# A two-layer encoder on one core: transfers, buffers and the order of products around a saturated TensorE

## The chip, the core and the metric

The kernel runs on one core of a Trainium2 chip. The metric is the device time of one execution in microseconds. Three runs of the kernel before gave 1870.45 us in the median (1870.34 to 1870.78).

## The reference, cut to what matters

Two layers of a macaron encoder over 512 tokens of width 1024, in float32: a half-step feed-forward part, gated parallel mixers (neighbourhood attention and a Fourier mix), a second half-step feed-forward part, and a norm at the very end.

```python
def swiglu(x, w_in, w_out):
    gu = x @ w_in
    g, u = jnp.split(gu, 2, axis=-1)
    return (jax.nn.silu(g) * u) @ w_out

def mixer(h, w_in, gate_bias, rpb, w_na_out, w_f_out, w_o):
    z = h @ w_in
...
    y_na = neighbourhood_attention(q.reshape(shp), k.reshape(shp), v.reshape(shp), rpb) @ w_na_out
    y_f = fourier_mix(uf) @ w_f_out
    g_na = jax.nn.sigmoid(ga + gate_bias[0])
    g_f = jax.nn.sigmoid(gf + gate_bias[1])
    return (g_na * y_na + g_f * y_f) @ w_o

def reference(x, ...):
    for l in range(DEPTH):
        x = x + 0.5 * swiglu(rms_norm(x, ffn1_norm[l]), ffn1_w_in[l], ffn1_w_out[l])
        x = x + mixer(rms_norm(x, mix_norm[l]), ...)
        x = x + 0.5 * swiglu(rms_norm(x, ffn2_norm[l]), ffn2_w_in[l], ffn2_w_out[l])
    return rms_norm(x, final_norm)
```

## The kernel before

**Products.** Every float32 operand is split into a high part (rounded, `hi`) and a low part (the rest, `lo`), and a product is three matmuls: high by high, high by low, low by high. ScalarE makes the high part of a weight tile (`Item.upper`, lines 196 and 198), VectorE the low part (`Item.lower`, lines 203 and 205). Large products are done in seven instead of eight block products (Strassen-like): with weight quarters a, b, c, d the products are numbered 1 to 7: 1 uses -a, 2 uses b, 5 uses d + c, 6 adds a to that tile, 3 adds b, 7 uses c + a, 4 uses d alone. Product 6 and 3 thus go on with the tile that product 5 began.

**Weight stream.** `stage_items` lists all weight granules (128 x 1024 floats, 512 KB) in the order in which TensorE uses them; `Stream` walks the list. `Raw.load` (lines 150 to 159) issues a granule's plain load on SyncE's queue and, for each granule that is to be added, a transfer with accumulation on POOL's queue. `fetch` loads 8 (feed-forward and second half of a mixer) or 4 items ahead of `high`; `high` makes the high part (and a sum on VectorE, line 191, where the item has an `add`), `low` the low part, and, where the item has a `then`, a further accumulating transfer onto the raw tile behind its split (line 215). Raw tiles of the feed-forward stages come from a pool of 9 buffers (`ffn_raw`, line 1811), split tiles from pools of 3.

In the feed-forward stages the sums of products 6 and 3 are made on VectorE from granules loaded by themselves. In the mixer's gate and output projections (`dma=True`) they are made by accumulating transfers. The output projection (`ORDER_W`) has a tile `s` of its own for products 6 and 3, which is d with c and then a added by two accumulating transfers; there are two such tiles, one for each half of the rows.

**The mixer's gates.** Two blocks of products (`block`, `block_1`), one for each half of the gates' columns, run interleaved as generators; the order in which `next` is called (lines 1740 to 1760) must be that of the items (line 288): ends with block 0's 6 and 7, block 1's 5, block 0's 3 and 4, block 1's 6, 7, 4, 3.

**End of the last feed-forward stage.** The output product of a stage goes over three thirds c of the hidden width. In the last layer (`late`) product 4's activations are made by a negation on ScalarE (line 1022) and an accumulating transfer on POOL (line 1023, the tile `at`). After product 7 of the last third the order of PE, VectorE and ScalarE is written out by hand in `end_part`: product 3's last granules, product 4 over its three thirds with the activations split in place (`upper`, its `lower`, lines 909 and 911), and interleaved the updates of x (line 730), the squares for the final norm (line 412), its roots, and the final scaling: `gained` multiplies by the gain (line 1063), `scaled` by the inverse norm and sends (lines 1068, 1069), `whole` does both at once (lines 1073, 1074).

**Start.** `ws.fetch(1)` issues the first granule in two halves on ScalarE's queue, then a small Silu brings in its table, while SyncE's queue loads the transposed x (`xt`) in five pieces with further granules between them (lines 1834 to 1856).

Of the kernel before, what the change touches and what calls it, by code (L numbers as in the profile page):

```python
# [17 lines left out]
P = 128  # L18
D = 1024
T = 512  # L20
L = 2
# [74 lines left out]
def encoder_kernel(  # L96
# [48 lines left out]

    class Raw:
# [3 lines left out]
        def load(self, parts=1):  # L150
            if self.t is None:
                self.t = raw_pool[0](self.n)
                for c in range(0, self.n, self.n // parts):
                    cs = slice(c, c + self.n // parts)
                    (S if parts > 1 else nc.sync).dma_start(out=self.t[:, cs], in_=wst[GRAN_AT[self.key]][:, cs])
                for plus in self.plus:
                    z = G.dma_start(out=self.t, in_=wst[GRAN_AT[plus]][:, 0 : self.n], accum_op=ALU.add)  # L157
                    if self.key[1:] == ("gc", 1, 1):
                        tc.keep_in_program_order(z)

# [56 lines left out]
    def stage_items():  # L217
# [7 lines left out]
        def strassen(s, name, idx, sizes, order, dma=False):  # L225
# [9 lines left out]
            for m in order:  # L235
                for g in range(len(sizes)):
                    a, b, c, d = [r[q][g] for q in "abcd"]
                    if m == 1:
                        add(a, neg=True)
                    elif m == 2:  # L240
                        add(b)
                    elif m == 3:
                        add(r["s"][g] if "s" in r else d, None if dma else b)
                    elif m == 4:
                        add(d2[g])
                    elif m == 5:
# [10 lines left out]
        def ffn(s):  # L257
            first = not items
            for g in range(4):
                add(Raw((s, "cl", g)), parts=2 if first and g < 2 else 1, pieces=2 if first and g == 0 else 1)  # L260
            for j in range(NB):
                order = (1, 2, 5, 6, 7, 3, 4) if s == (0, 1) and j == 0 else (1, 5, 6, 2, 7, 3, 4)
                strassen(s, lambda q: q, j, (1024, 1024), order)
            for order in ((1,), (2,), (5, 6, 7, 3), (4,)):
                for c in range(3):
                    strassen(s, lambda q: "o" + q, c, out_sizes(c), order)

        for l in range(L):
# [19 lines left out]
            for i, order in ((0, (5,)), (1, (2,)), (0, (6, 7)), (1, (5,)), (0, (3, 4)), (1, (6, 7, 4, 3))):  # L288
# [319 lines left out]
    def stage_ffn(norm, nxt, late):  # L608
# [274 lines left out]
        def end_part(i):  # L883
# [33 lines left out]
            ws.high()  # L917
            nxt.squares(1, 1)
# [3 lines left out]
            lower = upper(i + 3)  # L922
# [10 lines left out]
            lower = upper(i + 4)  # L933
# [8 lines left out]
            lower()  # L942
# [14 lines left out]
            scaled(nxt, 2, 1)  # L957
            for z in chain:
# [9 lines left out]
            gained(3, 1)  # L968
# [3 lines left out]
            scaled(nxt, 3, 1)  # L972
# [14 lines left out]
        for i, (m, c, _) in enumerate(steps):  # L987
# [36 lines left out]
            if late and (m, c) == (7, 2):  # L1024
                end_part(i)
# [51 lines left out]
    def stage_mixer(l, norm, nxt):  # L1077
# [732 lines left out]
    def ffn_raw(n):  # L1810
        return scope_pool[0].tile([P, 1024], F32, tag="raw", name=nm("raw"), bufs=9)[:, 0:n]
# [22 lines left out]
    ws.fetch(1)  # L1834
    S.activation(small("rt", 1), ones, AF.Silu)
    with tc.manual_schedule(engines={mybir.EngineType.SP}):
        for kts in ((0,), (1,), (2, 3), (4, 5), (6, 7)):
# [8 lines left out]
            src = src.rearrange("p (a b) -> p a b", b=T)  # L1846
            ws.fetch(kts[-1] // 2 + 1)
# [183 lines left out]
```

## Time and profile before

| | us |
|---|---|
| median of three runs | 1870.45 |
| profiled execution, its own time | 1872.14 |
| its span, first to last instruction | 1870.4 |
| TensorE busy | 1858.8 |
| VectorE busy | 1491.6 |
| ScalarE busy | 1176.1 |
| POOL busy | 182.5 |

The granted clock was 0.999 in the mean. In a row of a timeline the first number is the start in us from the span's start, the second the duration; then engine, line, operation, tile written and tiles read, shapes and count; in brackets how long the engine was idle before it and what released it. PE is TensorE's matmuls, PEld its weight loads, DVE VectorE, ACT ScalarE, SPq, ACTq and POOLq the transfers that these engines issue. Rows of waits read: engine, tile and line that waited, what for, us in total, how often, longest.

### The profile page before, as it was taken

To read this page: it belongs to the slowest core of one execution; us is meant where nothing else is said; L and a number is where in the kernel's file an instruction comes from. 1 tells how busy PE (TensorE), PEld (TensorE's weight loads), DVE (VectorE), ACT (ScalarE), POOL (GpSimd) and SP (SyncE) were. 2 spreads that over 40 slices of the span, in tenths; PEclk is the share of its full clock that TensorE was granted. 3 is DMA by queue.
4 is the path that set the end of the run, shared out by engine and by line. 5 is a ranking of instruction groups with operands and counts; after the bars stand their busy time and mean duration, and the time that the engine had idled before them with its cause. 6 is when DMAs were issued, how large, how long until landed. Compare 5 with 4: busy or idle time off the path is not lost.

```text
span 1870.4 us, 25957 instructions
## 1 busy us (share of the span) xinstructions
PE 1858.8 (99%) x9609; PEld 1583.5 (85%) x9609; DVE 1491.6 (80%) x1831; ACT 1176.1 (63%) x1751; POOL 182.5 (10%) x219
## 2 busy tenths in 40 slices
PE   9999999999999999999999999999999999999998
PEld 7888888889998888888888888888899988888886
DVE  7777799758879777779967777996687787777898
ACT  6655665768657655566665556667676575555665
POOL 0101011100211000001000100101002110100010
PEclk9999999999999999999999999999999999999999
DMA  9777488774998477659857774979659885765695
GB/s 301 204 197 198 151 238 272 249 205 121 253 241 231 133 206 184 182 154 264 242 141 198 198 183 148 262 226 279 196 142 248 231 232 144 191 182 163 180 272 181
DMA packets 110319, 384.57 MB, mean 206 GB/s; under 512 B 12512, under 2 KB 12640, under 8 KB 110192
## 3 DMA queue, kind: packets, MB, share of 16 engines
q1 hardware_dynamic: 79952, 276.81, 42.1%
q0 software_dynamic: 29808, 105.32, 30.7%
q8 instruction: 75, 1.23, 0.3%
q10 hardware_dynamic: 432, 0.79, 0.1%
q14 instruction: 52, 0.43, 0.1%
HBM read 375.13 MB, written 6.29 MB: 204 GB/s over the span
## 4 chain that ended last, share of the span: by engine, by line
PE 93%; DMA 2%; DVE 2%; issue 1%; ACT 1%; POOL 0%; ACTq 0%; POOLq 0%; DVEq 0%
PE A L367 9%; PE A L370 9%; PE A L368 9%; PE o L370 7%; PE o L367 7%; PE o L368 7%; PE B L367 5%; PE B L368 5%; PE B L370 5%; PE ps L367 3%; PE ps L368 3%; PE ps L370 3%; PE C L367 2%; PE C L370 2%; PE C L368 2%; PE tr L624 2%
## 5 line engine op out<-in xcount | busy, mean ns | idle before, releaser
L205 DVE TENSOR_TENSOR wlo<-raw,whi 128x1024 fp32r<-128x1024 f32 (+2 forms) x524 | 619.1, 1189 | 227.0 <-ACT whi L198 224.5
L198 ACT ACTIVATE whi<-raw 128x1024 fp32r<-128x1024 f32 (+2 forms) x524 | 537.5, 1032 | 340.6 <-PE A L368 128.7
L157 POOL DMA_DIRECT2D raw<-in_wst_dram x170 | 147.3, 879 | 1434.0 <-DMA raw<-in_wst_dram 824.9
L191 DVE TENSOR_TENSOR raw<-raw,raw 128x1024 f32<-128x1024 f32 (+1 forms) x128 | 151.3, 1187 | 2.4
L367 PE MATMUL A<-whi,xh 128*128 128x512 f32 x320 | 124.5, 389 | 0.0
L368 PE MATMUL A<-whi,xl 128*128 128x512 f32 x320 | 124.5, 389 | 0.0
L705 ACT ACTIVATE th<-sn,r 128x512 f32<-128x512 f32 x80 | 57.0, 715 | 73.6 <-DVE sn L606 73.6
L196 ACT ACTIVATE whi<-raw 128x1024 fp32r<-128x1024 f32 x76 | 78.8, 1037 | 34.4 <-issue 17.1
L203 DVE SCALAR_TENSOR_TENSOR wlo<-raw,whi 128x1024 fp32r<-128x1024 f32 x76 | 90.5, 1190 | 8.1 <-ACT whi L196 8.0
L370 PE MATMUL A<-wlo,xh 128*128 128x512 f32 x320 | 92.1, 389 | 0.0
L601 ACT ACTIVATE sn<-A 128x512 f32<-128x512 f32 x96 | 56.1, 590 | 46.0 <-PE A L370 46.0
L368 PEld LDWEIGHTS A<-whi,xl 128*128 128x128 f32 x320 | 60.1, 188 | 12.5
L370 PEld LDWEIGHTS A<-wlo,xh 128*128 128x128 f32 x320 | 60.1, 188 | 12.5
L367 PEld LDWEIGHTS A<-whi,xh 128*128 128x128 f32 x320 | 60.1, 188 | 12.5
L367 PE MATMUL B<-whi,t1h 128*128 128x512 f32 x160 | 63.7, 398 | 0.0
L367 PE MATMUL A<-whi,t2h 128*128 128x512 f32 x160 | 62.5, 391 | 0.0
L367 PE MATMUL B<-whi,xh 128*128 128x512 f32 x160 | 62.4, 390 | 0.0
L368 PE MATMUL B<-whi,xl 128*128 128x512 f32 x160 | 62.3, 390 | 0.0
L368 PE MATMUL B<-whi,t1l 128*128 128x512 f32 x160 | 62.3, 390 | 0.0
L368 PE MATMUL A<-whi,t2l 128*128 128x512 f32 x160 | 62.3, 389 | 0.0
L368 PE MATMUL A<-whi,t3l 128*128 128x512 f32 x160 | 62.2, 389 | 0.0
L367 PE MATMUL C<-whi,xh 128*128 128x512 f32 x160 | 62.2, 389 | 0.0
(454 smaller groups left out, 4895.4 us busy)
## 6 DMA issues: line engine op xcount, KB each, us to landing
raw<-in_wst_dram SPq DMA_DIRECT2D x463, 512.0 KB
raw<-in_wst_dram POOLq DMA_DIRECT2D x184, 512.0 KB, 8.1
raw<-in_wst_dram SPq DMA_DIRECT2D x28, 256.0 KB
vc<-vd SPq DMA_DIRECT2D x28, 256.0 KB
bm<-in_near_dram SPq DMA_DIRECT2D x16, 384.0 KB
vd<-v SPq DMA_DIRECT2D x8, 512.0 KB
dft<-in_dft_dram POOLq DMA_DIRECT2D x4, 514.0 KB, 10.2
x<-in_xin_dram SPq DMA_DIRECT2D x4, 512.0 KB
```

The lines of the kernel that those rows point to most:

```text
L157: z = G.dma_start(out=self.t, in_=wst[GRAN_AT[plus]][:, 0 : self.n], accum_op=ALU.add)
L191: V.tensor_tensor(self.raw.t, self.raw.t, self.add.t, ALU.add)
L196: S.activation(self.out[0][:, cs], self.raw.t[:, cs], AF.Copy, scale=-1.0)
L198: S.activation(self.out[0][:, cs], self.raw.t[:, cs], AF.Copy)
L203: self.last = V.scalar_tensor_tensor(lo, t, -1.0, hi.bitcast(F32), ALU.mult, ALU.subtract)
L205: self.last = V.tensor_tensor(lo, t, hi.bitcast(F32), ALU.subtract)
L367: PE.matmul(ps, lh, rh, start=start, stop=False, skip_group_check=again)
L368: PE.matmul(ps, *((lh, rl) if w == "l" else (ll, rh)), start=False, stop=False, skip_group_check=again)
L370: PE.matmul(ps, *((ll, rh) if w == "l" else (lh, rl)), start=False, stop=stop, skip_group_check=again)
L601: S.activation(t[:, b, :], ps[b], AF.Copy)
L624: PE.transpose(tr[:, k, b * P : (b + 1) * P], a[:, b, (q + k) * P : (q + k + 1) * P], ident)
L705: S.activation(th[:, b, :], g[:, b, :], AF.Silu, scale=norm.r[:, c : c + 1])
```

## The change

- `Raw.load` issues only the first accumulating transfer at once; a second one is put off until the next raw tile that is loaded has issued its own first one (`pending`). Only the tiles `s` of the output projection have two.
- The first granule's first half goes out on SyncE's queue, behind the first piece of `xt`, its second half on ScalarE's queue, behind the small Silu.
- The raw pool has 10 buffers.
- In the last output product, last third (`end`), product 3's sum is made by an accumulating transfer behind product 6's split, instead of on VectorE.
- In both layers the gates' products end in another order: block 0's 6, block 1's 5, block 0's 7 and 3, block 1's 6, block 0's 4, block 1's 7, 4, 3.
- In `end_part` product 4's second activations are split before the hand-written order begins (`make(i + 3)`), its third ones behind the first granule of product 3; `gained` and `scaled` for token block 3 come before the last block of products.

```diff
+    pending = []
...
-                    (S if parts > 1 else nc.sync).dma_start(out=self.t[:, cs], in_=wst[GRAN_AT[self.key]][:, cs])
-                for plus in self.plus:
-                    z = G.dma_start(out=self.t, in_=wst[GRAN_AT[plus]][:, 0 : self.n], accum_op=ALU.add)
+                    (S if c and parts > 1 else nc.sync).dma_start(out=self.t[:, cs], in_=wst[GRAN_AT[self.key]][:, cs])
+                for plus in self.plus[0:1]:
+                    z = self.gather(plus)
                     if self.key[1:] == ("gc", 1, 1):
                         tc.keep_in_program_order(z)
+                while pending:
+                    raw, plus = pending.pop(0)
+                    raw.gather(plus)
+                pending.extend((self, plus) for plus in self.plus[1:])
+
+        def gather(self, plus):
+            return G.dma_start(out=self.t, in_=wst[GRAN_AT[plus]][:, 0 : self.n], accum_op=ALU.add)
...
-                        add(r["s"][g] if "s" in r else d, None if dma else b)
+                        add(r["s"][g] if "s" in r else d, None if dma or end else b)
...
-                        add(t, None if dma else a, then=b.key if dma else None)
+                        add(t, None if dma else a, then=b.key if dma or end else None)
...
-                    strassen(s, lambda q: "o" + q, c, out_sizes(c), order)
+                    strassen(s, lambda q: "o" + q, c, out_sizes(c), order, end=(*s, c) == (L - 1, 2, 2))
...
-            for i, order in ((0, (5,)), (1, (2,)), (0, (6, 7)), (1, (5,)), (0, (3, 4)), (1, (6, 7, 4, 3))):
+            for i, order in ((0, (5,)), (1, (2,)), (0, (6,)), (1, (5,)), (0, (7, 3)), (1, (6,)), (0, (4,)), (1, (7, 4, 3))):
...
             go(p3, i + 1, 0, w[0])
             ws.high()
+            lower = upper(i + 4)
             nxt.squares(1, 1)
             ws.low()
             ws.high()
             go(p3, i + 1, 1, w[1])
-            lower = upper(i + 3)
             update(ps[1], 0, 1, -1)
...
             go(p4, i + 2, 1, ws.next(0))
-            lower = upper(i + 4)
...
             go(p4, i + 3, 0, ws.next(0))
-            lower()
...
             gained(2, 1)
             scaled(nxt, 2, 1)
+            gained(3, 1)
+            scaled(nxt, 3, 1)
...
-            gained(3, 1)
             whole(nxt, 2, 0)
             whole(nxt, 3, 0)
             next(chain[0])
-            scaled(nxt, 3, 1)
...
             if late and (m, c) == (7, 2):
+                make(i + 3)
                 end_part(i)
...
         written.pop().__exit__(None, None, None)
+        next(block_1)
+        next(block)
         next(block)
         next(block_1)
-        next(block)
         next(block)
...
-        return scope_pool[0].tile([P, 1024], F32, tag="raw", name=nm("raw"), bufs=9)[:, 0:n]
+        return scope_pool[0].tile([P, 1024], F32, tag="raw", name=nm("raw"), bufs=10)[:, 0:n]
...
-    ws.fetch(1)
-    S.activation(small("rt", 1), ones, AF.Silu)
...
+            if not kts[0]:
+                with tc.manual_schedule(engines={mybir.EngineType.SP, mybir.EngineType.Activation}):
+                    S.activation(small("rt", 1), ones, AF.Silu)
+                    ws.fetch(1)
```

More of the change, by code (lines that the diff above doesn't have):

```diff
@@ L223, in stage_items, with strassen @@
         made = {}
-        def strassen(s, name, idx, sizes, order, dma=False):
+        def strassen(s, name, idx, sizes, order, dma=False, end=False):
             r = made.setdefault((s, name("a"), idx), {}) if dma and len(order) < 7 and order[0] > 2 else {}
```

## The prediction

> **What bounds the kernel now.** I read the page first, then the busy time in stretches of 50 us, then TensorE's own waits, then the instructions around each place where TensorE (PE) stopped. The page says that PE is the whole story:
>
> ```profile
> span 1870.4 us, 25957 instructions
> PE 1858.8 (99%) x9609; PEld 1583.5 (85%) x9609; DVE 1491.6 (80%) x1831; ACT 1176.1 (63%) x1751; POOL 182.5 (10%) x219
> ```
>
> Only 1870.4 - 1858.8 = 11.6 us of the span have no matmul. Four rows of the stretches say where; the columns are PE, weight load, VectorE (DVE), ScalarE (ACT) and POOL busy, granted clock, DMA share, GB/s.
>
> ```profile
> 550.00:600.00 50.00, 50.00 (x239) 41.91 (x238) 44.66 (x52) 30.78 (x44) 7.32 (x9) 1.00 0.88 232
> 1500.00:1550.00 50.00, 49.07 (x232) 40.49 (x231) 45.21 (x52) 36.43 (x59) 5.18 (x6) 1.00 0.88 235
> 1800.00:1850.00 50.00, 49.58 (x218) 40.35 (x217) 46.60 (x47) 29.20 (x33) 6.97 (x8) 1.00 0.90 268
> 1850.00:1900.00 50.00, 12.75 (x57) 10.23 (x55) 15.93 (x36) 9.93 (x19) 0.00 (x0) 0.93 0.11 42
> ```
>
> PE stops for 50.00 - 49.07 = 0.93 us at the end of layer 1's mixer, where the same code in layer 0 (first row) loses nothing, and for 0.42 us late in the last feed-forward stage. After 1850 it works 12.75 us, so it is done near 1862.8, and 7.6 us of tail follow. The rest of the 11.6 us lies at the start. PE's waits, all four of them, agree:
>
> ```profile
> PE ps L143 <- DVE warm L140: 1.2, 1, 1.2
> PE cl L360 <- ACT whi L198: 1.2, 1, 1.2
> PE tr L452 <- DVE x L1802: 0.8, 1, 0.8
> PE o L370 <- DVE wlo L205: 0.4, 1, 0.4
> ```
>
> A busy PE is drawn with modelled ends, so the true loss is read from the starts of neighbours:
>
> ```profile
> 1528.09 0.27 PE L452 MATMUL tr<-ident,x 128*128 128x128 f32 x1
> 1529.20 0.66 PE L452 MATMUL tr<-ident,x 128*128 128x128 f32 x4 [0.84 <-DVE x L1802]
> ...
> 1806.46 0.39 PE L368 MATMUL o<-whi,c5l 128*128 128x512 f32 x1
> 1807.24 0.72 PE L370 MATMUL o<-wlo,c5h 128*128 128x512 f32 x2 [0.39 <-DVE wlo L205]
> ...
> 1839.82 0.39 PE L368 MATMUL o<-whi,c7l 128*128 128x512 f32 x1
> 1840.24 0.73 PE L370 MATMUL o<-wlo,c7h 128*128 128x512 f32 x2
> ...
> 1861.68 1.07 PE L370 MATMUL o<-wlo,c4h 128*128 128x512 f32 x4
> ```
>
> The last row gives the pitch of wide matmuls: (1.07 - 0.39) / 3 = 0.227 us. Transposes follow each other at (0.66 - 0.27) / 3 = 0.13. So the three stops cost 1.11 - 0.13 = 0.98 us; 0.78 - 0.23 = 0.55 and another 0.10 because the pair behind it takes 0.72 instead of 0.39 + 0.23, together 0.65; and 0.42 - 0.23 + 0.11 = 0.30. **The change adds and removes no matmul, so it can move the time only through these three stops, the start, the tail, and new stops that it makes.** That is some 2 us in the body and about as much at the ends, out of 1870.
>
> **The start.** Today ScalarE's queue issues both halves of the first weight granule before the Silu table is loaded. Afterwards SP issues the first half behind the first activations, and ScalarE issues the second half behind table load and Silu.
>
> ```profile
> 0.74 0.89 ACTq L155 DMA_DIRECT2D raw<-in_wst_dram  x2
> 1.67 1.28 ACT L1835 ACT_TABLE_LOAD   x1 [1.67 <-PEq L2021]
> 4.97 0.72 ACT L376 ACTIVATE xh<-xt 128x512 fp32r<-128x512 f32 x1 [1.80 <-DMA xt<-in_xtr_dram]
> 5.60 0.61 ACT L198 ACTIVATE whi<-raw 128x512 fp32r<-128x512 f32 x1
> 7.03 0.63 ACT L198 ACTIVATE whi<-raw 128x512 fp32r<-128x512 f32 x1 [0.82 <-DMA raw<-in_wst_dram]
> 9.62 0.19 PEld L368 LDWEIGHTS cl<-whi,xl 128*128 128x128 f32 x1 [0.54 <-DVE xl L377]
> ```
>
> The first matmul waits for the activations (4.97), their rounding (0.72) and the first half's rounding (0.61); the weight load at 9.62 then waits 0.54 us because the second half landed only at 7.03. Gain at most: PE's 1.2 us wait for the first rounding and these 0.5, so 1.7, if activations that share the engines with less come that much sooner. Loss at most: the second half goes out at 0.74 + 0.45 = 1.19 today and lands 5.84 us later; behind a table load started at 0.74 it goes out at 2.02 or later and would land 0.8 to 0.9 us later, all of it on the path. SP's later issues (the other activations, the next granules) each move back by one issue, 0.45 us, inside the same spread. No row decides between the ends, so I take the middle, **-0.4**.
>
> A rule of the Trainium skill speaks against this part (Trainium Kernel Development and Optimization, Key Constraints): transfers issued from SP, ScalarE and GpSimd run on the same 16 engines and interleave, so spreading the issuing over engines only saves issue time. By it nothing but one issue, 0.45 us, could be won and the late second half would be lost, which is rival 2 below; no run so far shows the other order.
>
> **Accumulating transfers interleaved (layer 1's output projection).** Two raw tiles are each a load plus two accumulating transfers on POOL's in-order queue. Today the order is c0, a0, c1, a1, and each a waits for its c to land with everything behind it:
>
> ```profile
> 1477.63 0.86 POOL L157 DMA_DIRECT2D raw<-in_wst_dram  x1 [6.25 <-DVE ga L1537]
> 1486.66 1.76 POOL L157 DMA_DIRECT2D raw<-in_wst_dram  x2 [8.17 <-DMA raw<-in_wst_dram]
> 1496.27 0.87 POOL L157 DMA_DIRECT2D raw<-in_wst_dram  x1 [7.85 <-DMA raw<-in_wst_dram]
> 1501.92 2.01 ACT L198 ACTIVATE whi<-raw 128x1024 fp32r<-128x1024 f32 x2 [2.01 <-DMA raw<-in_wst_dram]
> ```
>
> One wait of 8.17 us, then c1, then another of 7.85. In the order c0, c1, a0, a1 the second wait is gone: a1 goes out near 1488 instead of 1496.27. ScalarE's wait of 2.01 us at 1501.92 is for that tile, and everything later in the stage (the transfers that follow its split, the two last splits, the update of x that PE waits for at 1529.20) hangs on it. Layer 0 runs the same code with no idle PE, so about the whole stop is to be had: **-1.0**. Ends: 0 if the update of x is late for DVE's own load (45.21 of 50 busy), -1.0 otherwise; I take the full one because layer 0 has practically the same DVE load (44.66) and no stop.
>
> **Gates' products reordered.** Same products, same tiles; one block's product moves ahead of the other's, and the queues of SP and POOL carry the same granules in the new order, the sums by transfer keeping at least four granules between request and use. PE's four waits have none in the gate products, so there is nothing to gain; the smallest wait in that list, 0.4 us, bounds a loss or a gain hidden in the pitch. I take **0**. The cover is PE's own backlog of products; without it a late first product would cost that 0.4 in each of the two layers.
>
> **Ten raw buffers, and the last third product's sum by transfers.** In the last output product two DVE sums of 1.19 us go away, and their two plain loads become two accumulating transfers on POOL that start when the split of product 6's granule is done and must land before product 3 rounds the tile.
>
> ```profile
> L191 DVE TENSOR_TENSOR raw<-raw,raw 128x1024 f32<-128x1024 f32 (+1 forms) x128 | 151.3, 1187 | 2.4
> raw<-in_wst_dram POOLq DMA_DIRECT2D x184, 512.0 KB, 8.1
> ...
> 1788.31 1.23 POOL L1023 DMA_DIRECT2D at<-at  x1
> 1799.56 1.06 ACT L374 ACTIVATE c7h<-at 128x1024 fp32r<-128x1024 f32 x1 [1.78 <-DMA at<-at]
> 1826.46 0.86 POOL L157 DMA_DIRECT2D raw<-in_wst_dram  x1 [9.71 <-DMA raw<-in_wst_dram]
> 1834.25 1.06 ACT L198 ACTIVATE whi<-raw 128x1024 fp32r<-128x1024 f32 x1 [2.21 <-DMA raw<-in_wst_dram]
> 1837.87 2.01 ACT L198 ACTIVATE whi<-raw 128x1024 fp32r<-128x1024 f32 x2 [2.56 <-DMA raw<-in_wst_dram]
> 1830.78 2.52 DVE L205 TENSOR_TENSOR wlo<-raw,whi 128x1024 fp32r<-128x1024 f32 x2
> 1842.19 0.39 PE L367 MATMUL o<-whi,c3h 128*128 128x512 f32 x1
> at<-at POOLq DMA_DIRECT2D x1, 512.0 KB, 12.1
> ```
>
> The stop at 1807 goes back to ScalarE's 1.78 us behind a transfer that POOL issued late (1788.31), the one at 1840 to the 2.21 and 2.56 us behind loads whose accumulation POOL held for 9.71 us. A tenth buffer lets each load start one granule, 12 matmuls or 2.7 us, sooner. That exceeds all three waits, so I take both stops as gone: **-0.65 and -0.30**. Ends: 0, since the engines are already 0.90 busy there and bytes may not come sooner, and the full -0.95.
>
> The new wait: product 6's first split ends near 1830.78 + 1.26 = 1832.0 today. With 8.1 us to landing and 1.06 of rounding the tile is ready at 1841.2, against its first matmul at 1842.19, or 1841.2 once PE is 0.95 ahead. With the 12.1 us of the last row it is ready at 1845.2, 3.0 us after today's matmul. Splits are pulled ahead by the earlier loads, so I take a value near the short end, **+0.3** (ends 0 and 4.0, the latter with the 0.95 lost again). Behind the waiting rounding on ScalarE stand the other roundings of products 3 and 4, and PE waits for those.
>
> **The tail.** The multiplication and scaling by the final gain for the second half of token block 3 move ahead of the last products, and both remaining splits of the third product's activations move out of the stage's last third.
>
> ```profile
> 1849.01 1.22 DVE L911 TENSOR_TENSOR c4l<-at,c4h 128x1024 fp32r<-128x1024 f32 x1
> 1861.12 0.68 DVE L1063 TENSOR_TENSOR o<-x,gf 128x512 f32<-128x512 f32 x1
> 1863.23 0.67 DVE L730 SCALAR_TENSOR_TENSOR x<-o,x 128x512 f32<-128x512 f32 x1
> ```
>
> The last matmul ends near 1861.68 + 1.07 = 1862.75, its update starts at 1863.23: 0.48 us that DVE owes. The 0.68 us multiplication is taken from just ahead of it, but put ahead of the other half's update, so it helps only as far as DVE is early by then; 2.4 us of sums and a split of 1.2 us (L911) removed from the stage's end say that it is. Ends -0.48 and 0; **-0.3**. What follows the update is untouched.
>
> **Sum:** -0.4 - 1.0 + 0 - 0.65 - 0.30 + 0.3 - 0.3 = -2.35 us. The span is 1870.4 and the runs' median 1870.45, so they may be taken as one (the profiled execution itself took 1872.14, 1.7 us more than the median): 1868.1.
>
> **The rivals.**
> 1. The body as forecast and the start at its best, -1.7, with no new wait and the tail at -0.48: -1.7 - 1.0 - 0.95 - 0.48 = -4.1, 1866.3. For it: the activations are what the start waits for (1.80 us idle at 4.97). Against it: rounding two tiles, 1.3 us, stays on the path.
> 2. The second half comes late, start +0.9: -2.35 + 1.3 = -1.05, 1869.4. For it: the 1.28 us table load now stands ahead of that issue. Against: half as many bytes then share that queue.
> 3. The tenth buffer brings nothing because the engines are full (0.90): both late stops stay, -2.35 + 0.95 = -1.4, 1869.0. Against: full engines with waiting buffers still deliver in a better order.
> 4. **Slower:** the two sums by transfer land like the 12.1 us row, from a split no earlier than today's. PE then reaches product 3 3.0 us later than today, whatever it gained since 1800: -0.4 - 1.0 + 3.0 - 0.1 = +1.5, 1872.0. It decides from a landing of about 10.6 us on, where the total is zero. For it: three accumulating transfers then queue on POOL (the two sums, and the at tile's). Against: two of today's loads are gone from the engines, and the median is 8.1.
>
> **Chances.** Forecast 0.50 (1867.3 to 1868.8), rival 1 0.15, rival 2 0.12, rival 3 0.10, rival 4 0.13. The low end, 1866.2, is rival 1 with a tenth to spare; the high end, 1872.0, is rival 4. What a measurement of this kernel can tell from no change is about 0.2%, 3.7 us. Faster by more than that needs most of rival 1: 0.10. Slower by more needs rival 4 and a bad start together: 0.04. The rest, 0.86, lies within.
>
> **What would show it.** Right: PE's stop at 1529 gone, POOL issuing two accumulations before each long wait there; no ScalarE wait for the at transfer; no PE wait for weights near 1840; last update within 0.1 us of the last matmul. Wrong: ScalarE waiting for a raw tile ahead of product 3 (rival 4); the second rounding after 7.03 (rival 2); the waits of 2.21 and 2.56 still there (rival 3). The forecast falls altogether if PE shows a new stop in the gate products or anywhere before 1450.

## The result and the profile after

| | before | after |
|---|---|---|
| median of 22 executions, us | 1871.01 (1869.68 to 1874.1) | 1873.74 (1872.01 to 1876.11) |
| profiled execution, its own time | 1872.14 | 1873.27 |
| its span | 1870.4 | 1871.5 |

The ratio after to before is 1.0013, with a 95% interval of 1.0007 to 1.0019: **slower by about 2.4 us** (0.13% of 1871), with 1.3 to 3.6 inside the interval. The forecast was 1868.1 in a range of 1866.2 to 1872.0. The direction is wrong and the time lies outside the range, although it is within the 0.2% that was called no change.

The views of the changed kernel, in the order in which those of before were read. Line numbers have moved: 155 is now 157, 198 is 207, 205 is 214, 367 is 376, 370 is 379, 1023 is 1030, 1835 is 1856. First the waits of TensorE (what it waited for, us in total, how often, longest):

```profile
PE o L376 <- ACT whi L207: 1.3, 1, 1.3
PE cl L369 <- ACT whi L207: 1.3, 1, 1.3
PE ps L143 <- DVE warm L140: 1.2, 1, 1.2
PE o L379 <- DVE wlo L214: 0.7, 1, 0.7
PE A L376 <- ACT whi L207: 0.3, 1, 0.3
```

The wait for `x` at the end of the mixer is gone, as forecast. A wait of 1.3 us for a rounded weight in an output product has come, the wait for `wlo` has grown from 0.4 to 0.7, and there is a new one in the gate products (`A`). The stretches of 50 us say where (columns as before: PE, weight load, DVE, ACT, POOL, granted clock, DMA share, GB/s):

```profile
1500.00:1550.00 50.00, 50.00 (x237) 41.52 (x236) 46.36 (x53) 36.75 (x60) 5.20 (x6) 1.00 0.79 211
1800.00:1850.00 50.00, 47.83 (x208) 38.59 (x207) 43.55 (x44) 30.16 (x34) 8.72 (x10) 1.00 0.89 247
1850.00:1900.00 50.00, 14.05 (x63) 11.29 (x61) 16.79 (x37) 9.14 (x19) 0.00 (x0) 0.94 0.11 42
```

The first row was 49.07 busy and is 50.00. The second fell from 49.58 to 47.83, so the work that was left after 1850 grew from 12.75 to 14.05 us. PE lost 1.75 us more there than before and had 1.30 us more left afterwards; the difference it had won earlier. The timeline of PE shows the two places:

```profile
1802.07 0.39 PE L379 MATMUL o<-wlo,c3h 128*128 128x512 f32 x1
1802.59 0.50 PE L376 MATMUL o<-whi,c5h 128*128 128x512 f32 x1
1802.93 0.39 PE L377 MATMUL o<-whi,c5l 128*128 128x512 f32 x1
...
1806.14 0.39 PE L377 MATMUL o<-whi,c5l 128*128 128x512 f32 x1
1807.26 0.74 PE L379 MATMUL o<-wlo,c5h 128*128 128x512 f32 x2 [0.73 <-DVE wlo L214]
...
1841.43 0.61 PE L379 MATMUL o<-wlo,c7h 128*128 128x512 f32 x2
1843.35 0.50 PE L376 MATMUL o<-whi,c3h 128*128 128x512 f32 x1 [1.31 <-ACT whi L207]
1843.69 0.39 PE L377 MATMUL o<-whi,c3l 128*128 128x512 f32 x1
```

With the pitch of 0.227 us: 1802.07 to 1802.93 costs 0.86 - 0.45 = 0.41, 1806.14 to 1807.26 costs 0.89 and 0.12 more in the pair behind it, together 1.42 where before lost 0.65. Ahead of product 3 (`c3h`) the second matmul of the pair started at 1841.43 + 0.61 - 0.39 = 1841.65 (0.39 is one matmul's duration), so 1841.65 to 1843.69 costs 2.04 - 0.45 = 1.58, where before lost 0.30 in the same part of the program. The rows of ScalarE and POOL say what was late there:

```profile
1786.64 0.87 POOL L168 DMA_DIRECT2D raw<-in_wst_dram  x1 [0.35 <-DVE x L739]
1787.19 1.22 POOL L1030 DMA_DIRECT2D at<-at  x1
...
1825.85 1.22 POOL L1030 DMA_DIRECT2D at<-at  x1
1830.62 0.87 POOL L224 DMA_DIRECT2D raw<-in_wst_dram  x1 [3.56 <-DVE wlo L214]
1832.89 0.87 POOL L224 DMA_DIRECT2D raw<-in_wst_dram  x1 [1.41 <-DVE wlo L214]
...
1799.58 1.06 ACT L383 ACTIVATE c7h<-at 128x1024 fp32r<-128x1024 f32 x1 [2.57 <-DMA at<-at]
1842.25 1.06 ACT L207 ACTIVATE whi<-raw 128x1024 fp32r<-128x1024 f32 x1 [5.93 <-DMA raw<-in_wst_dram]
```

The first new sum (line 224) is issued at 1830.62 and its tile is rounded at 1842.25, 11.6 us later. ScalarE's wait for the `at` tile has grown from 1.78 to 2.57 us. The chain of waits (start, us, what) has both transfers among its longest pieces:

```profile
1787.19 12.38 DMA at<-at
1827.07 3.54 issue
1830.62 11.52 DMA raw<-in_wst_dram
```

The start of the changed kernel, in the timeline:

```profile
0.74 1.28 ACT L1856 ACT_TABLE_LOAD   x1 [0.74 <-PEq L2032]
0.91 0.39 ACTq L157 DMA_DIRECT2D raw<-in_wst_dram  x1
5.45 1.15 ACT L207 ACTIVATE whi<-raw 128x512 fp32r<-128x512 f32 x2 [0.69 <-DMA raw<-in_wst_dram]
6.13 1.20 PE L369 MATMUL cl<-whi,xh 128*128 128x512 f32 x4 [1.30 <-ACT whi L207]
```

ScalarE issues the second half at 0.91, while the table load is still running, and both halves are rounded one behind the other from 5.45 on. Last, the end:

```profile
1862.99 1.07 PE L379 MATMUL o<-wlo,c4h 128*128 128x512 f32 x4
1864.09 0.69 DVE L739 SCALAR_TENSOR_TENSOR x<-o,x 128x512 f32<-128x512 f32 x1
```

The last matmul ends near 1864.06 and its update follows after 0.03 us instead of 0.48.

The two profiles can be balanced from the starts of neighbouring matmuls: for each stage I sum what every distance over 0.24 us has above 0.227.

| difference after - before | us |
|---|---|
| first product of the kernel (6.26 to 6.13) | -0.13 |
| gaps up to 64 us (0.94 to 0.53) | -0.41 |
| gate products of both layers (0 to 0.50 and 0.28) | +0.78 |
| end of layer 1's mixer (1.59 to 0.57) | -1.02 |
| 1770 to 1830 (0.66 to 1.42) | +0.76 |
| from 1830 (0.31 to 1.58) | +1.27 |
| from the last matmul's start to the end (8.01 to 7.80) | -0.21 |
| sum; the spans differ by 1871.5 - 1870.4 = 1.1 | +1.04 |

Two profiles thus differ by 1.1 us, and the medians by 2.7. Before's profiled execution was itself 1.1 us above its kernel's median, the changed kernel's 0.5 below. The experiments look for the causes.

### The profile page after: what moved, and what is told of

Read it like the earlier page. It is cut to its first block, busy times and chain, and to the rows that moved or that the text cites. A ratio compares the mean times of both kernels' runs of the same rounds, so it can differ in the third digit from the quotient of the medians.

```text
span 1871.5 us, 25958 instructions
## 1 busy us (share of the span) xinstructions
PE 1858.8 (99%) x9609; PEld 1583.4 (85%) x9609; DVE 1489.1 (80%) x1829; ACT 1175.6 (63%) x1751; POOL 185.0 (10%) x221
## 3 DMA queue, kind: packets, MB, share of 16 engines
q1 hardware_dynamic: 79808, 276.02, 42.3%
## 4 chain that ended last, share of the span: by engine, by line
PE 96%; DMA 2%; DVE 1%; issue 0%; ACT 0%; POOL 0%; SPq 0%; POOLq 0%; ACTq 0%; DVEq 0%
PE A L376 9%; PE A L377 9%; PE A L379 9%; PE o L376 6%; PE o L377 6%; PE o L379 6%; PE B L376 5%; PE B L377 5%; PE B L379 5%; PE ps L376 3%; PE ps L377 3%; PE ps L379 3%; PE C L379 2%; PE C L376 2%; PE C L377 2%; PE tr L633 2%
## 5 line engine op out<-in xcount | busy, mean ns | idle before, releaser
L200 DVE TENSOR_TENSOR raw<-raw,raw 128x1024 f32<-128x1024 f32 x126 | 148.9, 1187 | 2.4
L376 PE MATMUL A<-whi,t3h 128*128 128x512 f32 x160 | 62.4, 390 | 0.0
```

Of the source, the lines that this page charges most:

```text
L200: V.tensor_tensor(self.raw.t, self.raw.t, self.add.t, ALU.add)
L376: PE.matmul(ps, lh, rh, start=start, stop=False, skip_group_check=again)
```

## The experiments

Each kernel has its ratio to the kernel before, measured side by side on one chip, with its 95% interval (the median of eleven executions, of seven for the kernel with the sum alone), and one profile. A and B are the sums of the balance above for 1770 to 1830 and from 1830 on, "gates" the sum for the gate products of both layers, in that one profile, in us.

| kernel | ratio, 95% interval | A | B | gates |
|---|---|---|---|---|
| the changed kernel again | 1.0008, 0.9999 to 1.0017 | 1.48 | 1.50 | 0.25 |
| sum on VectorE | 1.0001, 0.9992 to 1.0010 | 2.43 | 0.00 | 0.77 |
| gates as before | 1.0017, 1.0008 to 1.0026 | 1.55 | 0.55 | 0 |
| sum on VectorE, gates as before | 1.0002, 0.9994 to 1.0011 | 1.10 | 0.00 | 0 |
| nine buffers | 1.0021, 1.0012 to 1.0030 | 0.68 | 4.14 | 0 |
| not interleaved | 1.0011, 1.0002 to 1.0020 | 1.56 | 0.42 | 0.62 |
| nine buffers, sum on VectorE, gates as before | 1.0000, 0.9991 to 1.0009 | 1.29 | 0.27 | 0 |
| the same with 11 warming matmuls | 0.9995, 0.9986 to 1.0004 | 0.69 | 1.48 | 0 |
| start as before | 1.0015, 1.0005 to 1.0024 | 1.75 | 0.48 | 0.11 |
| before again | 0.9997, 0.9988 to 1.0006 | 1.03 | 0.00 | 0 |
| before, 11 warming matmuls | 0.9995, 0.9986 to 1.0004 | 0.00 | 0.17 | 0 |
| before, interleaved | 1.0003, 0.9994 to 1.0012 | 0.00 | 0.22 | 0 |
| before, ten buffers | 1.0002, 0.9993 to 1.0011 | 0.75 | 0.00 | 0 |
| before, gates reordered | 0.9997, 0.9988 to 1.0006 | 0.85 | 1.14 | 0 |
| before, sum by transfer | 1.0028, 1.0017 to 1.0039 | 0.38 | 6.69 | 0 |
| last `at` on VectorE | 1.0003, 0.9995 to 1.0012 | 1.52 | 0.00 | 0.50 |
| last `at` on VectorE, gates as before, 11 warming matmuls | 0.9999, 0.9990 to 1.0008 | 1.38 | 0.00 | 0.41 |
| all `at` on VectorE, gates as before, 11 warming matmuls | 0.9991, 0.9982 to 1.0000 | 0.00 | 0.00 | 0.03 |

Two of the entries at B, 1.14 and 1.48 with nine buffers and no sum by transfer, lie in product 7, like the 0.30 of before, and not ahead of product 3. Nor is A one place. With ten buffers all that is lost at A lies between 1798 and 1811, and it is there in ten of eleven profiles. With nine buffers something is lost there in three of nine profiles (0.66, 0.74 and 0.22); what else these have at A, as the 1.03 of the unchanged kernel, lies between 1811 and 1830.

**The changed kernel again.** No edit.

> The changed kernel once more, beside the three that follow. Its profile has TensorE stop 1.58 us ahead of product 3's first granule, 1.6 us in two stops near 1802 and 1806, and 0.5 and 0.2 us in layer 0's gate products. Theory A (the sum by transfers and the gates' order make the loss): the same places stop in every execution, with a spread of 1 to 2 us in size, and the time is 1.5 to 3.5 us above the kernel before. Theory B (the tenth buffer crowds the transfers, so every accumulating transfer lands later): the same here.

1.0008: 1.35 us above the kernel before, a little less than expected, and the interval just includes no change. The stops are at the same places, but for the first of the two in each layer's gates, which is missing. The profile had one thing more: its first products ran at half speed.

**The sum by transfer, taken away and done alone.** The first edit puts product 3's sum back on VectorE in the changed kernel; the other way round, only that part of the change was put into the kernel before.

```diff
-                    strassen(s, lambda q: "o" + q, c, out_sizes(c), order, end=(*s, c) == (L - 1, 2, 2))
+                    strassen(s, lambda q: "o" + q, c, out_sizes(c), order, end=False)
```

> Product 3's sum back on VectorE, all else as changed. Theory A: the stop ahead of product 3 goes (1.58 us), so the time is 1.3 to 2 us under the changed kernel; the stops near 1802 and in the gates stay. Theory B: product 3 stops no longer, but the two plain loads come late in its place and the time falls by under 0.7 us.

> The kernel before, nine buffers, with product 3's sum by transfer and nothing else. Theory A: a stop of 2 to 4 us ahead of product 3's granules near 1840, as in the changed kernel with nine buffers (4.1 us), and 2 to 4 us above the kernel before. If the stop is below 1 us, the other edits of the changed kernel (the moved splits) are needed to make it.

Without the sum by transfer the stop at B is gone (1.50 to 0.00) and the median falls from 1873.46 to 1872.17, 1.3 us, as expected, though the two intervals overlap. With it alone the kernel is slower by 0.28%, clear of noise and more than the 2 to 4 us expected (5.8 between the medians), and the timeline of that kernel (nine buffers) has the stop ahead of product 3 in full:

```profile
1831.93 0.87 POOL L215 DMA_DIRECT2D raw<-in_wst_dram  x1 [2.13 <-DVE wlo L205]
...
1845.31 1.06 ACT L198 ACTIVATE whi<-raw 128x1024 fp32r<-128x1024 f32 x1 [6.13 <-DMA raw<-in_wst_dram]
...
1841.98 0.61 PE L370 MATMUL o<-wlo,c7h 128*128 128x512 f32 x2
1846.42 0.50 PE L367 MATMUL o<-whi,c3h 128*128 128x512 f32 x1 [3.82 <-ACT whi L198]
...
1848.91 1.91 PE L370 MATMUL o<-wlo,c3h 128*128 128x512 f32 x4
1850.62 0.63 PE L367 MATMUL o<-whi,c3h 128*128 128x512 f32 x1
```

From issue to rounding it takes 13.4 us, PE stands for 3.82 us, and soon behind it the matmuls follow each other at (1850.62 - 1848.91) / 4 = 0.43 us instead of 0.23. The stretches of the same profile say that this is the clock:

```profile
1847.00:1852.00 5.00, 5.00 (x16) 3.96 (x15) 3.69 (x5) 3.21 (x6) 0.00 (x0) 0.66 0.00 1
1852.00:1857.00 5.00, 5.00 (x23) 4.13 (x22) 5.00 (x8) 3.44 (x8) 0.00 (x0) 1.00 0.00 0
```

The seventh value, the granted clock, is 0.66 behind the stop and 1.00 again 5 us later. The stop thus costs more than its length: of the 6.69 us at B 1.0 lies in product 7, and 5.7 belong to the 3.82 us of waiting and what the clock added.

**The number of buffers.** Nine instead of ten in the changed kernel, ten instead of nine in the kernel before, and nine without sum and new gates.

```diff
-        return scope_pool[0].tile([P, 1024], F32, tag="raw", name=nm("raw"), bufs=10)[:, 0:n]
+        return scope_pool[0].tile([P, 1024], F32, tag="raw", name=nm("raw"), bufs=9)[:, 0:n]
```

> Nine raw buffers, all else as changed. In the kernels with ten, POOL issues two weight accumulations right ahead of the first at transfer (1785.4 and 1786.6, then at 1787.2), which lands 12.4 us later; in the kernel before only one stood ahead of it and it landed in 11.2. Theory B (tenth buffer): the second accumulation falls back behind the at transfer, that lands within 11.5 us, the two stops near 1802 and 1806 shrink from 1.4 to about 0.7 us; the time is 0.7 us under the changed kernel, still about 1 above the kernel before because of the stop at product 3. Theory A (only the sum and the gates cost): the stops near 1802 stay at 1.4.

> The kernel before with ten raw buffers and nothing else. Theory B: a second weight accumulation goes out ahead of the first at transfer, that lands 12 us or more after its issue, TensorE stops 1.1 to 2.4 us between 1800 and 1808 (0 to 1.0 in the profiles with nine buffers), and the time is 0.5 to 1.5 us above the kernel before. Theory A: no difference, stops as in the kernel before.

> Nine buffers, sum on VectorE, gates in the old order: what is left of the change is the interleaving, the start and the hand-written end. Theories A and B together: no stop in the gates, none at 1529, 0.7 us near 1806, 0.3 or less near 1840; 1.0 to 1.8 us under the kernel before. If it is no better than the kernel before, the interleaving's 1.0 us is given back at some place that must then show in its profile.

The tenth buffer does two things, of opposite sign. In the kernel with the sum by transfer the stop at B is shorter with it (4.14 in the one profile with nine, 0.42 to 1.58 in five with ten), so that nine buffers, expected to be 0.7 us faster, were not. And the tenth buffer brings the stop near 1802 to 1807: with nine the changed kernel loses nothing between 1798 and 1811 (its 0.68 at A lies later), with ten 1.42 to 1.75. With nine the timeline of POOL has the `at` transfer between two weight sums,

```profile
1784.73 0.86 POOL L168 DMA_DIRECT2D raw<-in_wst_dram  x1 [9.17 <-PE o L379]
1785.27 1.22 POOL L1030 DMA_DIRECT2D at<-at  x1
1787.98 0.86 POOL L168 DMA_DIRECT2D raw<-in_wst_dram  x1 [1.50 <-DVE wlo L214]
```

and with ten (the rows of the changed kernel at 1786.64 and 1787.19 above) both weight sums go first: the second tile no longer waits for a free buffer. The `at` transfer then landed 12.38 us after its issue. In the kernel before with ten buffers alone the order is the same, the stop at A is 0.75, and the ratio 1.0002: nothing is won. That is rival 3, though not for its reason: the bytes came sooner, and in a worse order. Nine buffers with the sum on VectorE and the old gates, expected 1.0 to 1.8 us under the kernel before, are level with it (1.0000): what is then left of the change wins nothing that the times can tell.

**The interleaving**, taken away and done alone.

```diff
-                for plus in self.plus[0:1]:
+                for plus in self.plus:
                     z = self.gather(plus)
                     if self.key[1:] == ("gc", 1, 1):
                         tc.keep_in_program_order(z)
-                while pending:
-                    raw, plus = pending.pop(0)
-                    raw.gather(plus)
-                pending.extend((self, plus) for plus in self.plus[1:])
```

> The two accumulations of the output projection's tiles in the old order, all else as changed. If the interleaving is what removed the stop at 1529, it comes back with 0.8 to 1.0 us in layer 1 and the time is that much above the changed kernel. If the gates' order or the tenth buffer removed it, TensorE's records there stay as in the changed kernel.

> The kernel before with nothing but the interleaved accumulations. As forecast: the stop at 1529 and the one at 1534 gone, 1.0 us under the kernel before. Rival: the stop is not there in most executions of the kernel before, and the time is the same within 0.1%.

> The kernel before, unchanged, as one of the kernels compared: the ratio is that of no change, 1.000, and its interval is the resolution of these comparisons, about 0.1%. Its profile tells which of the three stops of the first profile are there in every execution. If the stop at 1529 is missing here, the 1.0 us that the forecast gave to the interleaving was the size of one execution.

The stop at 1529 is in none of the three, although the first and the third issue the two sums in the old order. In the unchanged kernel profiled again the stretch and the timeline read:

```profile
1500.00:1550.00 50.00, 50.00 (x238) 41.51 (x237) 46.35 (x53) 37.46 (x60) 5.18 (x6) 1.00 0.88 231
```

```profile
1529.11 1.03 PE L452 MATMUL tr<-ident,x 128*128 128x128 f32 x8
```

Eight transposes without a break, where the first profile had a gap of 0.84 us. That stop belonged to one execution, not to the kernel. Interleaving alone gives 1.0003, not interleaving 1.0011 against 1.0013 with it; a difference of the 1.0 us forecast, 0.05%, is below what these intervals of 0.09% either way can tell, so it is the profiles that decide. They also show that the long waits on POOL's queue did not go. In the kernel with nothing but the interleaving they read

```profile
1483.43 1.75 POOL L168 DMA_DIRECT2D raw<-in_wst_dram  x2 [7.33 <-DMA raw<-in_wst_dram]
1495.03 0.87 POOL L168 DMA_DIRECT2D raw<-in_wst_dram  x1 [9.85 <-DMA raw<-in_wst_dram]
```

where the unchanged kernel profiled again has 6.75 and 7.82 us. In the changed kernel the waits there are 6.69 and 2.92 us, but they are 6.67 and 2.97 without the interleaving; the second is also short with ten buffers alone (4.17 and 2.74) and with the new gates alone (3.65 and 3.25).

**The gates.** The old order in the changed kernel, with the sum and without, and the new order alone. The edit is the line of the diff that lists the orders (and the `next` calls that follow it):

```diff
-            for i, order in ((0, (5,)), (1, (2,)), (0, (6,)), (1, (5,)), (0, (7, 3)), (1, (6,)), (0, (4,)), (1, (7, 4, 3))):
+            for i, order in ((0, (5,)), (1, (2,)), (0, (6, 7)), (1, (5,)), (0, (3, 4)), (1, (6, 7, 4, 3))):
```

> The gates' products in the order of before, all else as changed. Theory A: TensorE has no stop in the gate products of either layer (0.5 and 0.2 us in layer 0, 0.3 and 0.2 in layer 1 gone), the time is 0.7 to 1.2 us under the changed kernel, and ScalarE no longer waits 3.1, 0.8 and 2.0 us for raw tiles there. Theory B: the stops stay, because the transfers land late with ten buffers in any order.

> Both put back: sum on VectorE, gates in the old order; interleaving, start, ten buffers and the end's new order stay. Theory A: the two gains add, 2 to 3 us under the changed kernel and 0.5 to 1.5 us under the kernel before, since the interleaved transfers (1.0 us) and the start (0.3 us) stay won. Theory B: no better than the kernel before.

> The kernel before with the gates' products in the new order and nothing else. The changed kernel with nine buffers has no stop in its gate products, with ten it has 0.1 to 0.8 us. If both are needed: no stop here, and the time of the kernel before within 0.1%. If the order alone makes it: 0.3 to 0.8 us of stops near 529, 541, 1458 and 1470.

The new order alone has no stop, nor has it with nine buffers; the old order with ten had 0, 0, 0, 0.03 and 0.41 (this last a wait for another instruction of ScalarE, not for a weight). With ten and the new order the stops are 0.11 to 0.78. The median does not follow: with the old gates the changed kernel stays at 1.0017, where 0.7 to 1.2 us less were expected. With sum and gates undone together it is 1.0002, as with the sum undone alone, and not under the kernel before as expected.

**The start.** As before in the changed kernel; and two more warming matmuls ahead of the first product (line 143), in the kernel before and in the one with nine buffers and no sum.

```diff
-                    (S if c and parts > 1 else nc.sync).dma_start(out=self.t[:, cs], in_=wst[GRAN_AT[self.key]][:, cs])
+                    (S if parts > 1 else nc.sync).dma_start(out=self.t[:, cs], in_=wst[GRAN_AT[self.key]][:, cs])
...
+    ws.fetch(1)
+    S.activation(small("rt", 1), ones, AF.Silu)
...
-            if not kts[0]:
-                with tc.manual_schedule(engines={mybir.EngineType.SP, mybir.EngineType.Activation}):
-                    S.activation(small("rt", 1), ones, AF.Silu)
-                    ws.fetch(1)
```

```diff
-WARM = 9
+WARM = 11
```

> Both halves of the first granule on ScalarE's queue ahead of the table load, all else as changed. First matmul at 6.2 to 6.3 us instead of 6.1 to 6.2, the wait of 0.5 us near 9.6 is back; 0.3 to 0.5 us above the changed kernel, which the times cannot tell but the records can. Where the first real matmuls follow each other at 0.43 us instead of 0.23 (as in two of the profiles with the new start), the same must be seen with this start if it is a matter of the clock and not of the order.

> The kernel before with 11 instead of 9 warming matmuls. In four of nine profiles the first 8 to 10 real matmuls follow each other at 0.43 us instead of 0.23, which costs 1.6 to 2.0 us, after a pause of 1.5 us behind the warming ones. If the pause sets the clock back, two more fill it (0.85 us): the cold start becomes rarer, the median falls by 0.3 to 1 us and the spread shrinks. If the clock depends on something else, nothing changes, or the first matmul comes up to 0.2 us later.

> Nine buffers, sum on VectorE, gates in the old order, with 11 warming matmuls: what is left of the change with a longer warm-up. If both theories hold (interleaving 0 to 1.0, start 0.3, warm-up 0.3 to 1) it is 0.5 to 2 us under the kernel before, the fastest so far.

With the old start the first product begins at 6.22 and the gap near 9 is back:

```profile
9.07 0.39 PE L376 MATMUL cl<-whi,xh 128*128 128x512 f32 x1
9.78 0.50 PE L377 MATMUL cl<-whi,xl 128*128 128x512 f32 x1 [0.32 <-DVE xl L386]
```

so the new start is worth 6.22 - 6.13 = 0.09 plus the gaps of 1.11 - 0.53 = 0.58, about 0.7 us, in these profiles. Some executions give it back: in the changed kernel's second profile the first products read

```profile
6.22 2.08 PE L369 MATMUL cl<-whi,xh 128*128 128x512 f32 x4 [0.97 <-ACT whi L207]
8.09 1.91 PE L371 MATMUL cl<-whi,xl 128*128 128x512 f32 x4
```

2.08 us for four matmuls, where the row of its first profile above has 1.20. Seven to ten matmuls run so in such a start, which costs 1.6 to 2 us. The stretch of that profile has a granted clock of 1.00 all the same, with 10 matmuls in 4.5 us:

```profile
6.00:10.50 4.50, 4.28 (x10) 3.45 (x11) 4.30 (x10) 3.46 (x7) 0.00 (x0) 1.00 1.01 382
```

Among the profiles with nine warming matmuls this was so in 4 of 9 with the new start and in none of 7 with the old one; with 11 it was so in none of 4. So few profiles do not settle whether the new start brings it. The medians do not show it, nor a gain from the longer warming that is clear of noise: start as before 1.0015; 1.0000 and 0.9995 without and with the longer warming; 0.9995 with it in the kernel before.

**What stands ahead on POOL's queue.** The `at` transfer of the last third is issued 4.8 us ahead of the sum on the same queue (1825.85 above); the sum's issue itself waits for VectorE's split. In these three kernels the difference that makes `at` is taken on VectorE: in the last third only (the first two of them), or in all three thirds. The second and the third also have the old gates and 11 warming matmuls. The edit, in the last third or in each:

```diff
-                S.activation(t, t, AF.Copy, scale=-1.0)
-                G.dma_start(out=t, in_=part(1, 0, c), accum_op=ALU.add)
+                V.tensor_tensor(t, part(1, 0, c), t, ALU.subtract)
```

> The changed kernel with the last third's at difference made on VectorE (one subtraction of 1.2 us) instead of ScalarE and an accumulating transfer, so that no 512 KB transfer stands on POOL's queue right ahead of the two sums. If the sums land late because they queue behind it: they land in about 8 us instead of 11.5, and the stop ahead of product 3 (0.4 to 1.6 us) goes; 0.5 to 1.5 us under the changed kernel. Rival: the sums land late because the plain loads fill the engines; then they still take 11 us and the stop stays.

> The same with only the last at difference on VectorE. No stop at product 3 and in the gates, 1.4 us near 1802 stay: 1 to 2 us under the changed kernel, level with the kernel before or up to 1 us under it.

> The changed kernel with all three at differences on VectorE, the gates in the old order and 11 warming matmuls. If the at transfers on POOL's queue are behind both the stops near 1802 (VectorE's c7 waits for their landing) and the one at product 3, both go; VectorE has 3.6 us more to do between 1780 and 1840, 2.4 of which the sum by transfer took away. 1.5 to 3 us under the changed kernel, 0.5 to 1.5 under the kernel before. If VectorE is the bound there, new stops of 1 us and more for split weights show instead, and nothing is won.

With the last one on VectorE and the sum still by transfer, POOL and ScalarE read:

```profile
1824.12 0.87 POOL L168 DMA_DIRECT2D raw<-in_wst_dram  x1 [0.42 <-issue]
1830.39 0.87 POOL L224 DMA_DIRECT2D raw<-in_wst_dram  x1 [5.40 <-DVE wlo L214]
...
1838.14 1.06 ACT L207 ACTIVATE whi<-raw 128x1024 fp32r<-128x1024 f32 x1 [2.22 <-DMA raw<-in_wst_dram]
```

The sum is issued at the same time as in the changed kernel (1830.39 against 1830.62) and its tile is rounded after 7.75 us, 7.86 in the second of the three, instead of 10.4 to 11.6 in the five profiles with ten buffers and the transfer; the stop at B is 0.00 in both kernels that do this, while the stop at A stays (1.52 and 1.38). With all three on VectorE both stops are gone. PE's waits of that kernel, all of them, and its stretch are

```profile
PE ps L143 <- DVE warm L140: 1.2, 1, 1.2
```

```profile
1800.00:1850.00 50.00, 50.00 (x222) 41.42 (x221) 49.20 (x53) 29.68 (x37) 5.19 (x6) 1.00 0.73 202
```

The only wait left is the one ahead of the warming matmuls, the engines of the transfers are busy 0.73 of the time instead of 0.89, and VectorE, now at 49.20 of 50, holds nothing up. **This version is the fastest of all:** 1870.06 us in the median (1869.6 to 1871.57) against 1871.70 for before in the same comparison, 0.9991 with an interval up to 1.0000, so that a gain over before is not quite clear of noise. From the second of the three it differs in the first two `at` transfers alone. That one had 1872.34 in the same comparison: the median is 2.28 us lower without them, and the slowest execution, 1871.57, lies under seven of the other's eleven.

## Why the prediction was wrong, step by step

**The new wait, "+0.3 (ends 0 and 4.0)"**, is the step that failed most. It is the mechanism of rival 4, and it was mis-sized by choosing the short landing: 0.3 us forecast, 1.58 in the first profile. I put 8.1 us, the median of all sums by transfer, against 12.1 for the `at` transfer. I chose near the short end because "splits are pulled ahead by the earlier loads", and held against rival 4 that "two of today's loads are gone from the engines". The split did come sooner (issue at 1830.62 instead of 1832.0), but the landing was long. From issue to rounding it took 10.4 to 11.6 us in the changed kernel with ten buffers, 13.4 with the sum alone, and 7.75 once the `at` transfer was out of the way. The median came from the whole program; at this place the nearest row was the 12.1 one, and that very transfer stands ahead in the same queue. The stop was 0.4 to 1.6 us in five profiles with ten buffers, and about 4 in the two with nine (2.9 and 1.1 ahead of product 3's two granules in the changed kernel, 4.0 without what the clock added in the kernel before). All seven comparisons in which the sum goes by transfer behind an `at` transfer lie at 1.0008 to 1.0028; all that lack either lie at 0.9991 to 1.0003. Whether the `at` transfer delays the sum by its place in the queue or by the engine time that it takes was not separated.

**Interleaving, -1.0**, fell altogether. The stop to be removed was one execution's, and the step that was to remove it, "the second wait is gone", failed too: with the interleaving alone POOL still waits 7.33 and then 9.85 us. The second wait shrinks with ten buffers or with the new gates, for a reason that stays open. The comparison with layer 0 was the hint, read the wrong way: the same code without a stop showed that the stop was not the code's, before it showed that it could be had.

**Ten buffers, -0.65 and -0.30**, fell too. The stops of before at 1807 and 1840 also change from execution to execution: its five profiles with nine buffers and no sum by transfer (the first, the repetition, longer warming, interleaving alone, gates alone) have 0.66, 1.03, 0, 0 and 0.85 at A, and the 1.03 lies at 1817 and 1829. And an earlier load has a side that I did not cost: it puts a further sum ahead of the `at` transfer, for which ScalarE then waits 2.57 us instead of 1.78. I had named that wait as the cause of the stop at 1807, but counted the buffer only as time won. With ten buffers the stop at A was there in every profile (0.75 to 2.43) but the one without `at` transfers.

**The gates, 0**, hold for the median as far as it can tell. But the profiles show 0.1 to 0.8 us where new order and ten buffers meet, and the first one's 0.50 in layer 0 is over the bound of 0.4 for a layer. A new stop in the gate products was named as the sign by which the forecast falls altogether, and it came: PE's backlog did not cover the new order together with the tenth buffer.

**The start, -0.4**: about -0.55 to -0.7 in the profiles, near the middle chosen. Rival 2 is refuted: the row at 0.91 shows the transfer issued inside the table load's 0.74 to 2.02, so "2.02 or later" was wrong, and the two halves are rounded without a break from 5.45 on, where before the second waited until 7.03. The Trainium skill (Trainium Kernel Development and Optimization, Key Constraints) says that issuing from several engines only saves issue time; one issue is 0.45 us here. The measured 0.55 to 0.7 is a little more, and as the order of the transfers changed too, these runs do not test the rule.

**The tail, -0.3**: -0.21 between the two profiles, and the update follows the last matmul at once, as forecast. But it does so in the unchanged kernel profiled again (after 0.05 us), whose tail is 7.58 us, and with the change the tail is 7.59 to 8.00: a gain is not shown.

**The balance.** With the terms as measured, against an ordinary execution of before without the 1529 stop: start -0.54, interleaving 0, gates +0.78, A +0.76, B +1.27, tail -0.21, together +2.06 us, which fits the 1.3 to 3.6 of the ratio. It is one profile's sum; of the parts of the change, the times single out only the sum by transfer. The forecast also started from a median of three executions, 1870.45; that of twenty-two is 1871.01.

## What to carry to other kernels

A stop of a microsecond in one profile is priced as a gain only when a second execution has it too; here 2 of the 2.35 us forecast were stops that came and went. When a sum moves from an engine to an accumulating transfer, its landing is taken from the transfers at that place and from what stands ahead of them in the queue, not from the median of the program. A deeper prefetch can let background transfers overtake one that an engine is waiting for, so it should be asked which of the queue's entries is urgent; here taking the urgent ones off the queue, even onto an engine with little to spare, was worth 2.28 us in the median, and the buffer nothing.

## What the runs showed of the hardware

**The accumulating transfers took the engines about twice as long per byte as the plain ones.** The queues of the kernel before from 1776 to 1850 (packets, MB, share of 16 engines; POOL's is q0, SP's is q1):

```profile
q0 software_dynamic: 1872, 6.42, 45.6%
q1 hardware_dynamic: 3610, 12.60, 44.7%
```

45.6 / 6.42 = 7.1% per MB against 44.7 / 12.60 = 3.5%; in the kernel without any `at` transfer the sums alone have the same 7.1% (42.3% for 5.97 MB). So moving two granules from plain loads to sums by transfer took nothing off the engines, against what I argued for the short landing: by these shares two granules, 1.05 MB, are 0.071 x 1.05 x 74 = 5.5 us of all engines as sums, 2.7 as loads.

**The clock fell after a stop of 3.82 us in a stream that had run for 1.8 ms.** The matmuls behind the stop first kept their 0.23 us; from 1847.7 on, 1.3 us after they had resumed, they ran at 0.43 for 3 us. The Trainium skill (TensorE: Matmul & The Clock Gate, Part 1: The HAM clock gate) states half rate after an idle window of about 3.4 us, with a window that runs free of the kernel. The 0.43 against 0.23 agrees, and a stop of 2.61 us, the next longest in these runs, was followed by no slow matmul. Whether the slow starts have the same cause is not shown: the granted clock of the one looked at reads 1.00, so that only the spacing of the matmuls shows it.
